# Weight sums of the two-by-two products, made by adding transfers

## The chip, the cores and the metric

The kernel runs on one core of one Trainium2 chip. A core has five engines that run side by side, each with its own queue of instructions, worked off in order: TensorE (PE; matmuls, with the weight loads PEld beside them), VectorE (DVE), ScalarE (ACT), GpSimd (POOL) and SyncE (SP), which here only issues transfers. Transfers issued by any of them run on the core's 16 DMA engines. They wait for each other by semaphores; a framework that lays out the program sets these from what each instruction reads and writes.

The metric is the device time of one execution in microseconds. The kernel before took 825.94 us as the median of three runs (825.88 to 827.58).

## The reference

One layer of an encoder over 512 positions of width 1024, all in float32:

```
h  = rmsnorm(x) * g_pre_mix
q, k, v, g, u, sv, a_ret, a_sgu = split(h @ w_in)
y_ret = (layernorm(retention(q, k, v), both directions) * silu(g)) @ w_ret_o
y_sgu = (gelu(u) * (spatial mixing of layernorm(gelu(sv)))) @ w_sgu_o
merged = sigmoid(a_ret) * y_ret + sigmoid(a_sgu) * y_sgu
x1 = x  + rmsnorm(merged @ w_out) * g_post_mix
y  = x1 + rmsnorm(conv-gated MLP(rmsnorm(x1) * g_pre_ffn)) * g_post_ffn
```

The MLP has a projection up to 2 x 2816 channels, a convolution of width 3 over the positions, gelu(a) * b, and a projection down. Only the matrix products with large weights matter here: `h @ w_in`, the two output projections, `w_out`, `w_up` and `w_down`.

## The kernel before

**Number format.** Every weight tile and every activation is split into a high part (rounded to the format that TensorE multiplies at full rate) and a low part (the rest), and a product is three matmuls: high x high, high x low, low x high. The split (`split`, L84) is one ACT copy (L79) and one VectorE subtraction (L86). So each weight that comes from memory costs ACT and VectorE one pass each before TensorE may use it.

**Weights.** All weights lie in one tensor `wall` of 146 blocks of 128 x 1024 (512 KB). A block is loaded by SP into one of four `raw` tiles and split from there into slots of the pool `w4` (nine of them). `w_get` (L203) hands out the next weight and, while there is room, prepares those that come after it, so splits run ahead of TensorE until the nine slots are full; then a split waits for the matmuls that free a slot.

**Pairs.** For u, for the two gates and for most of the projection up, two blocks of output channels are computed together as one product of two-by-two block matrices with seven products in place of eight (a Strassen-Winograd scheme; `Pair`, L676). The activations come as eight forms (parts of x and the sums S1 to S4), and the weights as seven forms of 128 x 512, in this order:

```
FORMS = ("B11", "B21", "T1", "T2", "T3", "T4", "B22")
```

Here B11, B12, B21, B22 are quarters of the pair's weights, and T1 = B11 + B12, T3 = B12 + B22, T2 = T1 + B22, T4 = T2 + B21. `w_form` (L156) makes them. There are twenty pairs: four of u, eight of the gates, eight couples of the projection up. A pair of u has nothing else beside it; a pair of the gates or of the projection up has two ordinary blocks of weights beside it (`pair[:4]`, block, `pair[4:]`, block, L101 and L106).

A pair's seven products (`part1`: B11, B21, T1, T2; `part2`: T3; `part3`: T4, B22) write to three PSUM banks. Several products add to the same bank: after B11's product ACT copies the bank out (`c0`), T2's product then adds to it, ACT copies again (`c1`), T3's product adds, ACT copies, T4's product adds. Each of these matmuls must wait for the copy before it. For u the `part3` of a pair comes after the `part1` of the next pair.

In the kernel before, the form B11 starts two loads by SP (L160, L161) into raw tiles a and b. The form T1 takes a third raw tile t; VectorE adds T1 and T3 (L167, L168), GpSimd adds T2 (L169), and with the form T4 GpSimd adds T4 (L171). Then each form is split.

**Order.** Each engine's order comes from the framework's scheduler, which starts from the order of the program. GpSimd also does the reciprocal roots of the norms (L322, L325), four loads of xT (L658) just before u, the additions that join the two branches in the second gates (L806), and a few broadcasts. TensorE comes from the product for the gate g into the pairs of u at about 216 us, into the first gates at about 253 us, the second gates at about 367 us, and the couples of the projection up at 520 us.

Of the kernel before, what the change touches and what calls it, by code (L numbers as in the profile page):

```python
# [13 lines left out]
ALU = mybir.AluOpType  # L14

P = 128
D = 1024
S = 512
# [29 lines left out]
def tile_block(ctx: ExitStack, tc, xT, x, wall, par, cs, wsp, bsp, gpost, gffn, out):  # L48
    nc = tc.nc
# [6 lines left out]
    def nm(s):  # L56
        uid[0] += 1
        return f"{s}_{uid[0]}"

    def blk(dt=F32, n="blk", shape=(P, S)):  # L60
        return sb.tile(list(shape), dt, tag="blk", bufs=NBLK, name=nm(n))

    def tmp(n="tmp", shape=(P, S)):
        return sb.tile(list(shape), F32, tag="tmp", bufs=6, name=nm(n))
# [19 lines left out]
    def split(hi, lo, src):  # L84
        copy(hi, src)
        nc.vector.tensor_sub(lo, src, as32(hi))  # L86
# [7 lines left out]
    i = 0  # L94
    while i < NW:
# [7 lines left out]
        elif i == UP0 + 2 * COUPLES[0][0]:  # L103
# [3 lines left out]
            i = UP0 + 2 * COUPLES[-1][1] + 2  # L107
# [10 lines left out]
    w_ready, w_pos, w_held, w_raw = {}, [0, 0], [0], {}  # L118

    def raw_tile():  # L120
        return sb.tile([P, 1024], F32, tag="raw", bufs=4, name=nm("raw"))
# [4 lines left out]
    def slot(n, at=0, w=1024):  # L126
        return sb.tile([P, 1088], F32R, tag="w4", bufs=9, name=nm(n))[:, at : at + w]
# [28 lines left out]
    def w_form(form, i):  # L156

        if form == "B11":
            a, b = raw_tile(), raw_tile()
            nc.sync.dma_start(a, wall[i])  # L160
            nc.sync.dma_start(b, wall[i + 1])  # L161
            w_raw["B11"], w_raw["B12"] = a[:, :S], a[:, S:]
            w_raw["B22"], w_raw["B21"] = b[:, :S], b[:, S:]
        elif form == "T1":
            t = raw_tile()
            w_raw["T1"], w_raw["T2"], w_raw["T3"], w_raw["T4"] = t[:, :S], t[:, S:], w_raw["B12"], t[:, S:]
            nc.vector.tensor_add(w_raw["T1"], w_raw["B11"], w_raw["B12"])  # L167
            nc.vector.tensor_add(w_raw["T3"], w_raw["B12"], w_raw["B22"])  # L168
            nc.gpsimd.tensor_tensor(out=w_raw["T2"], in0=w_raw["T1"], in1=w_raw["B22"], op=ALU.add)  # L169
        elif form == "T4":  # L170
            nc.gpsimd.tensor_tensor(out=w_raw["T4"], in0=w_raw["T2"], in1=w_raw["B21"], op=ALU.add)  # L171
        w = slot("wf", 0, 1088)
        lo, hi = w[:, AT_64 : AT_64 + S], w[:, S + AT_192 : 2 * S + AT_192]
        split(hi, lo, w_raw[form])
        return hi, lo
# [21 lines left out]
    def w_unit(u):  # L197
        return w_block(u[1]) if u[0] == "blk" else (w_down if u[0] in "qt" else w_form)(*u)
# [67 lines left out]
    for k in range(KD):  # L266
# [18 lines left out]
        for m in range(8):  # L285
            c = slice(m * P, (m + 1) * P)
# [5 lines left out]
    T0, T1 = slice(0, 256), slice(256, 512)  # L292
# [35 lines left out]
    for t in range(NT):  # L328
        for n in range(2):
# [3 lines left out]
                out=xt, in_=xt, func=AF.Square, accum_out=ss[:, 4 * n + t : 4 * n + t + 1]  # L333
# [19 lines left out]
    for c in range(19, 1, -2):  # L353
        v.scalar_tensor_tensor(
            out=lc, in0=lc, scalar=1.0 / c, in1=lb, op0=ALU.add, op1=ALU.mult
# [4 lines left out]
        out=lg, in0=lc, scalar=-2.0, in1=lg, op0=ALU.mult, op1=ALU.add  # L360
# [5 lines left out]
    for m in range(8):  # L366
        t = blk(n="qkraw")
# [286 lines left out]
    for n, acc in enumerate(t_group()):  # L654
        if n < 2:
            for k in (n + 2, n + 6):
                t = tmp("xT")
# [83 lines left out]
    for j in range(KD // 2):  # L741
        p = Pair(AF.Gelu_apprx_tanh, lambda: blk(n="u"), None, rbc)
# [52 lines left out]
    for j in range(KD // 2):  # L795
        for o, t in gated_pair(ogh, ogl, late if j == 0 else None):
            b = blk(n="r")
# [221 lines left out]
    i = 0  # L1019
    while i < NF:  # L1020
        if i in couples:
            p = Pair(None, lambda: tmp("c"), (h2h, h2l, h2forms))
# [179 lines left out]
def _parts(a, n, w):  # L1202

    k = a.shape[0] // P
    return a.reshape(k, P, n, w).transpose(2, 1, 0, 3).reshape(n, P, k * w)
# [15 lines left out]
def _two(a):  # L1221

    b = _parts(a, 8, P).reshape(4, 2, P, 2, S)
    return np.stack([
        np.concatenate([b[:, 0, :, 0], b[:, 1, :, 0]], -1), np.concatenate([b[:, 1, :, 1], b[:, 0, :, 1]], -1),
    ], 1)


def _up(a):

    for i, _ in COUPLES:
        b, c = a[2 * i].reshape(P, 2, S), a[2 * i + 1].reshape(P, 2, S)
        a[2 * i : 2 * i + 2] = np.stack([
            np.concatenate([b[:, 0], c[:, 0]], -1), np.concatenate([c[:, 1], b[:, 1]], -1),
        ])
    return a


def _gates(a, w):

    return np.concatenate([_two(a), _parts(w, 8, P).reshape(4, 2, P, 1024)], 1).reshape(16, P, 1024)
# [79 lines left out]
```

## Time and profile before

| what | value |
|---|---|
| median of three runs | 825.94 us (825.88 to 827.58) |
| the profiled execution | 827.49 us, of which the span of the profile is 825.7 us |
| granted TensorE clock | 0.999 |
| busy: TensorE, VectorE, ScalarE, GpSimd | 815.4, 661.4, 440.8, 101.0 us |
| HBM read, written | 88.19 MB, 4.19 MB |
| loads of raw tiles by SP | 145 of 512 KB, median 3.6 us to landing |

Rows of a group read: line, engine, operation, what it writes and reads, shapes, count, then busy time in us and the mean of one in ns, then the engine's idle time just before and what ended it. The chain of work that ended last gives start, length and the piece; several instructions of one line in a row are one piece (x48: 48 of them). The timeline gives start, length, engine, line, and in brackets the idle time before and its end. A wait reads: who waited, for whom, total us, times, longest. A DMA issue gives count, size and the median time from issue to landing. Time runs from the span's start.

### The profile page before, as it was taken

What the parts mean: (1) busy time and instruction counts of PE and PEld (TensorE: products, weight loads), DVE (VectorE), ACT (ScalarE), POOL (GpSimd) and SP (SyncE); (2) the same over time, 40 slices, a digit from 0 to 9 for tenths busy, and PEclk for the clock granted to TensorE, in tenths of its full rate; (3) what the DMA queues carried; (4) which work ended last, traced back from release to release, by engine and by line L of the source; (5) the groups of instructions that cost most, each with busy time, mean ns of one, the idle gap of its engine ahead of it and who ended that gap; (6) DMA issues with size and microseconds to landing.
All of it is one profiled execution on the core that took longest, in us unless ns stands there. A gap on an engine that the chain in (4) does not pass through costs nothing.

```text
span 825.7 us, 13263 instructions
## 1 busy us (share of the span) xinstructions
PE 815.4 (99%) x5152; PEld 735.0 (89%) x5152; DVE 661.4 (80%) x1101; ACT 440.8 (53%) x771; POOL 101.0 (12%) x102
## 2 busy tenths in 40 slices
PE   9999999999999999999999999999999999999996
PEld 7888888888899999999988898899999998999996
DVE  7489897878797777767765568979899899988967
ACT  6636445546665444444445685556566566544531
POOL 0010000102121111132211211210111200000001
PEclk9999999999999999999999999999999999999999
DMA  8733222212223232222349111322322341233244
GB/s 294 246 116 102 77 77 77 77 52 78 90 102 129 103 102 80 101 101 103 108 166 339 48 55 55 103 102 103 102 103 102 102 154 52 77 115 129 96 147 154
DMA packets 29215, 93.24 MB, mean 113 GB/s; under 512 B 3360, under 2 KB 4000, under 8 KB 29152
## 3 DMA queue, kind: packets, MB, share of 16 engines
q1 hardware_dynamic: 26928, 86.85, 30.2%
q0 software_dynamic: 1360, 4.46, 1.6%
q10 hardware_dynamic: 864, 1.09, 0.4%
q8 instruction: 40, 0.66, 0.3%
q14 instruction: 23, 0.19, 0.1%
HBM read 88.19 MB, written 4.19 MB: 112 GB/s over the span
## 4 chain that ended last, share of the span: by engine, by line
PE 91%; DVE 6%; ACT 1%; issue 1%; DMA 0%; POOL 0%; DVEq 0%; SPq 0%; POOLq 0%; ACTq 0%
PE ps L692 23%; PE ps L217 12%; PE ps L218 12%; PE ps L219 12%; PE ps L1058 8%; PE ps L481 5%; PE ps L480 5%; PE ps L482 5%; PE ps L836 2%; PE ps L837 2%; PE ps L838 2%; PE ps L1074 1%; PE ps L761 1%; DVE fl L86 1%; PE ps L279 1%
## 5 line engine op out<-in xcount | busy, mean ns | idle before, releaser
L86 DVE TENSOR_TENSOR wl<-raw,wh 128x1024 fp32r<-128x1024 f32 (+1 forms) x93 | 109.1, 1182 | 48.9 <-PE ps L692 24.2
L79 ACT ACTIVATE wf<-raw 128x512 fp32r<-128x512 f32 x140 | 85.3, 627 | 102.7 <-PE ps L218 34.0
L86 DVE TENSOR_TENSOR wf<-raw,wf 128x512 fp32r<-128x512 f32 x140 | 111.1, 808 | 23.3 <-ACT wf L79 22.4
L692 PE MATMUL ps<-sh,wf 128*128 128x256 f32 x640 | 119.5, 277 | 0.0
L79 ACT ACTIVATE wh<-raw 128x1024 fp32r<-128x1024 f32 (+2 forms) x95 | 93.3, 993 | 37.4 <-DMA raw<-wall 17.0
L692 PEld LDWEIGHTS ps<-sh,wf 128*128 128x128 f32 x640 | 101.1, 188 | 0.8 <-ACT u L79 0.2
L217 PE MATMUL ps<-h2h,wh 128*128 128x512 f32 (+1 forms) x256 | 92.4, 363 | 0.7 <-ACT h2h L906 0.7
L218 PE MATMUL ps<-h2l,wh 128*128 128x512 f32 (+1 forms) x256 | 92.4, 363 | 0.0
L219 PE MATMUL ps<-h2h,wl 128*128 128x512 f32 (+1 forms) x256 | 92.1, 361 | 0.0
L692 PE MATMUL ps<-sl,wf 128*128 128x256 f32 x320 | 88.8, 278 | 0.0
L480 PE MATMUL ps<-wh,xh 128*128 128x512 f32 x192 | 75.0, 391 | 0.0
L481 PE MATMUL ps<-wl,xh 128*128 128x512 f32 x192 | 74.9, 390 | 0.0
L482 PE MATMUL ps<-wh,xl 128*128 128x512 f32 x192 | 74.8, 390 | 0.0
L169 POOL TENSOR_TENSOR raw<-raw,raw 128x512 f32<-128x512 f32 x20 | 36.2, 1809 | 235.2 <-DVE raw L167 207.8
L1058 PE MATMUL ps<-dl,fh 128*128 128x256 f32 x216 | 60.8, 281 | 0.1
L1058 PE MATMUL ps<-dh,fl 128*128 128x256 f32 x216 | 60.7, 281 | 0.0
L1058 PE MATMUL ps<-dh,fh 128*128 128x256 f32 x216 | 60.7, 281 | 0.0
L692 PEld LDWEIGHTS ps<-sl,wf 128*128 128x128 f32 x320 | 60.0, 188 | 0.6
L219 PEld LDWEIGHTS ps<-h2h,wl 128*128 128x128 f32 x256 | 48.0, 188 | 7.7
L217 PEld LDWEIGHTS ps<-h2h,wh 128*128 128x128 f32 x256 | 47.9, 188 | 7.9 <-ACT h2h L906 1.0
L692 PE MATMUL ps<-xh,wf 128*128 128x256 f32 x288 | 54.2, 278 | 0.0
L218 PEld LDWEIGHTS ps<-h2l,wh 128*128 128x128 f32 x256 | 48.0, 188 | 6.6
(314 smaller groups left out, 2048.9 us busy)
## 6 DMA issues: line engine op xcount, KB each, us to landing
raw<-wall SPq DMA_DIRECT2D x145, 512.0 KB, 3.6
x<-x SPq DMA_DIRECT2D x24, 256.0 KB, 5.9
xT<-xT SPq DMA_DIRECT2D x8, 256.0 KB, 5.4
x<-x POOLq DMA_DIRECT2D x8, 256.0 KB, 2.4
xT<-xT POOLq DMA_DIRECT2D x4, 256.0 KB, 3.6
out<-zg SPq DMA_DIRECT2D x4, 256.0 KB, 2.0
out<-zs ACTq DMA_DIRECT2D x3, 256.0 KB, 3.5
cs<-cs SPq DMA_DIRECT2D x2, 256.0 KB, 4.1
```

The lines of the kernel that those rows point to most:

```text
L79: nc.scalar.activation(out=o, in_=i, func=AF.Copy)
L86: nc.vector.tensor_sub(lo, src, as32(hi))
L169: nc.gpsimd.tensor_tensor(out=w_raw["T2"], in0=w_raw["T1"], in1=w_raw["B22"], op=ALU.add)
L217: nc.tensor.matmul(o, ah, bh, start=start, stop=False)
L218: nc.tensor.matmul(o, ah, bl, start=False, stop=False)
L219: nc.tensor.matmul(o, al, bh, start=False, stop=stop)
L480: nc.tensor.matmul(acc[t], xh[k][:, c], wh[:, f], start=k == 0, stop=False)
L481: nc.tensor.matmul(acc[t], xh[k][:, c], wl[:, f], start=False, stop=False)
L482: nc.tensor.matmul(acc[t], xl[k][:, c], wh[:, f], start=False, stop=k == KD - 1)
L692: nc.tensor.matmul(o, w_[:, c], a_, start=first and k == n == 0, stop=k == 3 and n == 2, skip_group_check=True,)
L836: nc.tensor.matmul(o, ah, bh, start=k == 0, stop=False)
L1058: nc.tensor.matmul(o, a_[:, c], w_[:, f], start=j == t == i == 0, stop=j == DP - 1 and i == 2 and n not in (M2, M3, M4), skip_group_check= ...
```

## The change

The weights are laid out otherwise in memory, so that a pair's first block is B11|B21 and its second is B12|B22 (`_two`, `_up`). With the form B11 three raw tiles are taken at once, t, a and b, in this order:

- SP loads t = B11|B12, the left halves of both blocks, by one transfer with two rows of 2 KB for each partition. GpSimd issues a transfer that adds the second block, B12|B22, to it: t = T1|T3.
- SP loads a = B11|B21.
- SP loads b = B22|B22, one half block read twice. GpSimd issues a transfer that adds T1, from t, to b's right half: b = B22|T2.
- With the form T1 GpSimd issues a transfer that adds T2, from b, to a's right half: a = B11|T4. It must wait until B21 has been split.

The four additions on VectorE and GpSimd are gone. The matmuls, the splits and the forms' order are the same. In the changed program GpSimd's queue has, for the pairs of u, the T1|T3 sum of the next pair ahead of the T4 sum of this one; for later pairs the three sums of a pair stand together. The first T1|T3 sum stands ahead of the last reciprocal root of the retention, the first T2 sum ahead of the loads of xT. TensorE's order of matmuls is the same; ScalarE's and VectorE's differ in a few neighbours. Below the changed lines, line numbers are one lower than before.

```diff
         if form == "B11":
-            a, b = raw_tile(), raw_tile()
+            t, a, b = raw_tile(), raw_tile(), raw_tile()
+            nc.sync.dma_start(t.rearrange("p (b c) -> p b c", b=2), wall[i : i + 2, :, :S].rearrange("b p c -> p b c"))
+            nc.gpsimd.dma_start(t, wall[i + 1], accum_op=ALU.add)
             nc.sync.dma_start(a, wall[i])
-            nc.sync.dma_start(b, wall[i + 1])
-            w_raw["B11"], w_raw["B12"] = a[:, :S], a[:, S:]
-            w_raw["B22"], w_raw["B21"] = b[:, :S], b[:, S:]
+            twice = wall[i + 1, :, None, S:].to_broadcast([P, 2, S])
+            nc.sync.dma_start(b.rearrange("p (b c) -> p b c", b=2), twice)
+            nc.gpsimd.dma_start(b[:, S:], t[:, :S], accum_op=ALU.add)
+            w_raw["T1"], w_raw["T3"] = t[:, :S], t[:, S:]
+            w_raw["B11"], w_raw["B21"] = a[:, :S], a[:, S:]
+            w_raw["B22"], w_raw["T2"], w_raw["T4"] = b[:, :S], b[:, S:], w_raw["B21"]
         elif form == "T1":
-            t = raw_tile()
-            w_raw["T1"], w_raw["T2"], w_raw["T3"], w_raw["T4"] = t[:, :S], t[:, S:], w_raw["B12"], t[:, S:]
-            nc.vector.tensor_add(w_raw["T1"], w_raw["B11"], w_raw["B12"])
-            nc.vector.tensor_add(w_raw["T3"], w_raw["B12"], w_raw["B22"])
-            nc.gpsimd.tensor_tensor(out=w_raw["T2"], in0=w_raw["T1"], in1=w_raw["B22"], op=ALU.add)
-        elif form == "T4":
-            nc.gpsimd.tensor_tensor(out=w_raw["T4"], in0=w_raw["T2"], in1=w_raw["B21"], op=ALU.add)
+            nc.gpsimd.dma_start(w_raw["T4"], w_raw["T2"], accum_op=ALU.add)
...
     return np.stack([
-        np.concatenate([b[:, 0, :, 0], b[:, 1, :, 0]], -1), np.concatenate([b[:, 1, :, 1], b[:, 0, :, 1]], -1),
+        np.concatenate([b[:, 0, :, 0], b[:, 0, :, 1]], -1), np.concatenate([b[:, 1, :, 0], b[:, 1, :, 1]], -1),
     ], 1)
...
         a[2 * i : 2 * i + 2] = np.stack([
-            np.concatenate([b[:, 0], c[:, 0]], -1), np.concatenate([c[:, 1], b[:, 1]], -1),
+            np.concatenate([b[:, 0], b[:, 1]], -1), np.concatenate([c[:, 0], c[:, 1]], -1),
         ])
```

In the changed kernel the three adding transfers are L161 (T1|T3), L165 (T2) and L170 (T4), the three loads L160, L162 and L164.

## The prediction

> **What bounds the kernel now.** I read the cores first, then the busy time per engine, then what TensorE waited for, and last the chain that ended last around the pairs.
>
> ```profile
> core 0: 825.7 us, clock 0.999
> PE 815.4 (99%) x5152; PEld 735.0 (89%) x5152; DVE 661.4 (80%) x1101; ACT 440.8 (53%) x771; POOL 101.0 (12%) x102
> PE ps L264 <- DVE raw L259: 1.0, 1, 1.0
> PE ps L217 <- ACT h2h L906: 0.7, 1, 0.7
> PE ps L624 <- DVE o L615: 0.3, 1, 0.3
> PE ps L605 <- DVE o L615: 0.3, 1, 0.3
> 216.77 5.92 PE ps L692 x52
> 222.72 39.74 PE ps L692 x332
> 561.55 5.45 PE ps L692 x48
> 582.05 5.45 PE ps L692 x48
> ```
>
> TensorE is busy for 815.4 of 825.7 us at full clock, and all that it waited for by name is a handful of waits of 1.0 us at most; the rest of its idle time is the end of the kernel. So work taken off VectorE or GpSimd is worth next to nothing as such. What the change can do is make TensorE wait. The place to look is where pairs follow one another fastest: the four pairs of u with the first four products of the gate run from 216.77 to 222.72 + 39.74 = 262.46, 384 matmuls in 45.7 us, so 32 products at 1.43 us and a pair in 10.0 us. A later pair has two ordinary blocks beside it: from the first products of one couple of up to those of the next it is 20.5 us (561.55 to 582.05).
>
> **What it removes.**
>
> ```profile
> L167 DVE TENSOR_TENSOR raw<-raw 128x512 f32<-128x512 f32 x20 | 13.8, 688 | 1.5 <-DMA raw<-wall 1.4
> L168 DVE TENSOR_TENSOR raw<-raw,raw 128x512 f32<-128x512 f32 x20 | 17.1, 853 | 1.0 <-DMA raw<-wall 0.7
> L169 POOL TENSOR_TENSOR raw<-raw,raw 128x512 f32<-128x512 f32 x20 | 36.2, 1809 | 235.2 <-DVE raw L167 207.8
> L171 POOL TENSOR_TENSOR raw<-raw,raw 128x512 f32<-128x512 f32 x20 | 26.7, 1333 | 75.2 <-DVE wf L86 71.4 <-ACT cv L955 3.9
> L86 DVE TENSOR_TENSOR wf<-raw,wf x140: 674/686/1782, 191.9 to 668.1; 128x512 fp32r<-128x512 f32 x140
> ```
>
> VectorE loses 13.8 + 17.1 = 30.9 us, GpSimd 36.2 + 26.7 = 62.9 us, and VectorE's splits no longer meet a GpSimd sum (686 ns is the usual split, 1782 the one beside such a sum). Of all this the path sees one thing: TensorE's wait of 0.3 us for L615, which has L167 and L168 ahead of it on VectorE. Gain: 0.3 us. What is late next there is the release of the slots by TensorE itself.
>
> **What it adds.** Per pair, SP issues three loads of 512 KB for two; GpSimd issues three adding transfers: T1|T3 (512 KB from wall, on t), T2 (256 KB, from t on b), T4 (256 KB, from b on a). Twenty pairs move 31 MB more.
>
> ```profile
> q1 hardware_dynamic: 26928, 86.85, 30.2%
> raw<-wall SPq DMA_DIRECT2D x145, 512.0 KB, 3.6
> x<-x POOLq DMA_DIRECT2D x8, 256.0 KB, 2.4
> xT<-xT POOLq DMA_DIRECT2D x4, 256.0 KB, 3.6
> DMA to landing us min/median/max: 3.3/3.6/6.8
> 188.00 2.38 POOL L658 DMA_DIRECT2D xT<-xT  x4
> ```
>
> 60 issues at 0.6 us (four in 2.38) are 36 us on a GpSimd that has just lost 62.9: hidden. Twenty more SP issues at 0.33 us fall on a queue that mostly waits. The engines stand at 30.2% of 825.7 us x 16 for 86.85 MB, or 45.9 engine-us per MB, so 512 KB takes 1.5 us on all sixteen; 31 MB more is no bound on the average. Latency is what counts.
>
> No transfer of before adds. Call x the time of the 256 KB one from issue to landing, X that of the 512 KB one. Ends for x: 2.4 (the GpSimd queue's stores, same size) and 6.8 (the slowest load of raw). I take x = 3.6, the GpSimd queue's row of the same size that also writes a tile: that it must read its target too (0.75 us by the rate above) and that its source is on the chip (2.4 against 3.6) roughly cancel. For X I take 3.6 + 1.5 = 5.1, the load of that size and its second read; ends 3.6 and 6.8. The Trainium skill, page "DMA: Bandwidth & Descriptors", section "Anatomy of one DMA", fits 2.0 us + bytes/436e3 for a transfer of this queue, which is 2.6 us for 256 KB. The xT row has 3.6 for that size, so the trace is a microsecond above it.
>
> **The pairs of u.** Four raw tiles turn in the order t, a, b, t, a, b, so b of a pair lies in the tile of the a before it, whose right half holds the former T4. That makes a ring: T4 is split, SP loads b into its place (3.6), GpSimd adds t (x), GpSimd adds it on a (x), the new T4 is split. On TensorE's side the ring has 10.0 us.
>
> ```profile
> 209.16 1.30 DVE L86 TENSOR_TENSOR wf<-raw,wf 128x512 fp32r<-128x512 f32 x2 [2.45 <-ACT wf L79]
> 222.56 0.62 ACT L79 ACTIVATE wf<-raw 128x512 fp32r<-128x512 f32 x1
> 223.22 0.69 DVE L86 TENSOR_TENSOR wf<-raw,wf 128x512 fp32r<-128x512 f32 x1 [0.20 <-ACT wf L79]
> 243.00 0.63 ACT L79 ACTIVATE wf<-raw 128x512 fp32r<-128x512 f32 x1 [0.42 <-POOL raw L171]
> 245.15 0.37 ACT L79 ACTIVATE u<-ps 128x256 f32<-128x256 f32 x1
> 256.05 0.37 ACT L79 ACTIVATE sig<-ps 128x256 f32<-128x256 f32 x1
> ```
>
> T4 of the first pair is split as before (209.16, the first of two), so the second pair's b can be loaded from 210; its T4 is split on time too, being summed by 213.6 + 2x = 220.8, before ACT wants it at 222.56. VectorE is done at 223.9, and from 224.0 on: third pair's T4 at 224.0 + 3.6 + 2x; with 1.5 for the two halves of the split and the hand-over, the fourth's at 224.0 + 2(3.6) + 1.5 + 4x = 232.7 + 4x, that of the first gate pair at 237.8 + 6x. At x = 3.6 these are 234.8, 247.1 and 259.4, where ACT had 243.00 for the fourth.
>
> TensorE uses T4 late, but ACT runs in order, and behind the T4 split stands the copy of the pair's first product out of its bank (245.15 and 256.05), which must be done before the T2 product adds to that bank. T2 of the fourth pair starts with matmul 264 of the 384, at 222.72 + 212 x 0.1197 = 248.1; T2 of the gate pair with 348, at 258.15. The fourth pair's copy ends 1.6 us after its T4 (splits of T4 and B22, then itself): 234.3 + 4x against 248.1. The gate pair's ends 1.05 after: 238.85 + 6x against 258.15. So TensorE loses 6x - 19.3 by then, if x is over 3.2: at x = 3.6 it is **2.3 us**; at 2.4 nothing, at 6.8 21.5. The splits themselves keep 1 us or more ahead of their products, so the copies are what is late.
>
> **The gates.** From the split of T4 it now goes: load of the next t (3.6), X, then x for T2, and behind the T2 split on ACT stands the copy of the T3 product, due before the T4 product (the x24 pieces of the chain).
>
> ```profile
> 300.55 0.68 DVE L86 TENSOR_TENSOR wf<-raw,wf 128x512 fp32r<-128x512 f32 x1
> 313.95 0.38 ACT L79 ACTIVATE sig<-ps 128x256 f32<-128x256 f32 x1 [0.44 <-PE ps L692]
> 316.66 2.73 PE ps L692 x24
> 387.12 3.00 POOL L806 TENSOR_TENSOR sig<-sig,r 128x512 f32<-128x512 f32 x2 [6.28 <-DVE sig L805]
> 389.00 0.33 SPq L161 DMA_DIRECT2D raw<-wall  x1
> 399.55 0.38 ACT L79 ACTIVATE sig<-ps 128x256 f32<-128x256 f32 x1 [0.39 <-PE ps L692]
> 402.26 2.73 PE ps L692 x24
> ```
>
> First four pairs: t can load from 301.3, lands 304.9; the copy must start by 316.2, the T2 split by 315.6: X + x may be 10.7. It is 5.1 + 3.6 = 8.7, and a and b loading at the same moment add perhaps 0.5: hidden. Second four, without the mixing of the SGU in between: t from 389.05 (where SP went on when the split was done), landed 392.65; T2 must be split from 401.2: X + x may be 8.55, and 9.2 is 0.65 too much, at three passages from pair to pair: **2.0 us**. GpSimd's sums of the branches (L806) end at 390.1, before it waits for t; behind its three transfers nothing else is due. On SP the load of b, waiting for its tile, holds back only the loads of the next tiles, which are wanted later.
>
> **The couples of up.** There the copy of the T3 product stands ahead of the splits of T1 and T2, and the couple lasts 20.5 us:
>
> ```profile
> 573.87 0.38 ACT L79 ACTIVATE c<-ps 128x256 f32<-128x256 f32 x1 [1.29 <-PE ps L692]
> 576.23 0.63 ACT L79 ACTIVATE wf<-raw 128x512 fp32r<-128x512 f32 x1 [1.24 <-POOL raw L169]
> ```
>
> T2's split at 576.23 is used only after the next couple begins, 582.05; I count nothing, up to about 4 us of delay.
>
> **Moved on GpSimd's queue.** Its first adding transfer stands ahead of a reciprocal root, its second ahead of the loads of xT.
>
> ```profile
> 171.01 0.33 SPq L160 DMA_DIRECT2D raw<-wall  x1
> 180.60 0.20 POOL L322 TENSOR_SCALAR rs<-mv 128x4 f32<-128x4 f32 x1 [16.11 <-DVE mv L559]
> 184.22 1.22 DVE L86 TENSOR_TENSOR wl<-raw,wh 128x1024 fp32r<-128x1024 f32 x1 [0.91 <-PE ps L481]
> 194.88 1.35 ACT L255 ACTIVATE xg<-xT,part 128x512 f32<-128x512 f32 x2
> ```
>
> t lands by 174.6, so the root is not held. b's tile comes free when the ordinary block before is split (184.22 + 1.22) and lands by 189.2, so xT goes out at 189.8 for 188.0 and lands by 193.4; ACT wants it at 194.88. Hidden, with 1.5 us left; beyond that every microsecond delays the forms of x.
>
> **Sum.** -0.3 + 2.3 + 2.0 = +4.0 us. The profiled execution took 827.49 us (span 825.7 and 1.8 around it), so 831.5 on its account; it lies at the top of the three runs (825.88 to 827.58). On their median, 825.94, it is 829.9.
>
> **Rivals.** *Hidden: no change.* An adding transfer takes 3.2 us or less and X + x no more than 8.0. The place is the ring of u: up to x = 3.2 it costs nothing, and only the 0.3 us is left: 825.6. For it: the GpSimd queue's stores, 2.4. Against it: the loads of that queue have 3.6, and this one reads two things. By the fit of the Trainium skill's page x would be 2.6, the ring would hide it, and the sum would be -0.3. *Slow adding.* The engines need four times the pass of a plain copy: x = 3.6 + 1.5 = 5.1, X = 3.6 + 3.0 = 6.6. Then u costs 11.3; the first gates 12.2 - 10.7 = 1.5 at four passages, 6; the second 3.65 at three, 11: 854. For it: nothing in this trace adds in flight, so nothing excludes it; against it, the loads are mostly fixed time (3.6, of which 1.5 moves bytes). *Faster.* VectorE and GpSimd get 94 us lighter. TensorE's waits after the start add up to 1.3 us (0.7, 0.3 and one of 0.3 more), so this ends at 824.6 at best, inside what can be told.
>
> **How the numbers follow.** Under 0.2% (1.65 us) a measurement can't tell this kernel from no change. Stalls as forecast 0.48 (its own range 827.6 to 842: x from 3.5 to 5), hidden 0.30, slow adding 0.17, faster 0.05. Slower is the first, the third and a little of the second: 0.67; same 0.29, with most of the rival that gains; faster 0.04. The range 825.2 to 845 leaves out most of the slow case and the gains.
>
> **What would show it.** L165 and L170 landing near 3.6 us and L161 near 5. ACT's wf splits of T4 released by a DMA around 235, 247 and 259, and TensorE waiting for ACT u and sig in L692, 2 to 3 us before 262; three waits for ACT sig between 380 and 425. VectorE near 610 us busy (661.4 less 30.9 and the stretched splits). Wrong, if the adding transfers land over 5 us (then waits in all gates), or if TensorE waits for wf itself, or if the xT forms are late before 216.

## The result, and the profile after

The changed kernel takes 868.81 us as the median of four runs (865.83 to 870.79), against 825.99 for the kernel before in the same comparison (825.88 to 827.58): 1.052 times as long, 95% interval 1.0479 to 1.056. The forecast was 829.9, with a range to 845. The profiled execution took 870.79 us, its span 869.0.

The busy rows of the changed kernel's page:

```profile
PE 830.3 (96%) x5152; PEld 745.1 (86%) x5152; DVE 617.0 (71%) x1061; ACT 438.7 (50%) x771; POOL 90.4 (10%) x122
```

What TensorE waited for by name (who, for whom, total us, times, longest):

```profile
PE ps L691 <- ACT c L79: 11.7, 7, 4.5
PE ps L691 <- ACT sig L79: 11.3, 7, 3.8
PE ps L691 <- ACT u L79: 6.0, 2, 3.9
PE ps L623 <- DVE o L614: 0.3, 1, 0.3
```

VectorE did get lighter (661.4 to 617.0). TensorE now waits 29 us for the copies of ScalarE out of the banks, in 16 stalls of u, the gates and up; none of these rows names a wf tile. The same matmuls also take 830.3 us instead of 815.4. The wait of 0.3 for the transposes (L623; L624 before) is still there.

Both kernels issue the same 5152 matmuls in the same order, so the start of the n-th in one trace less its start in the other says how late a stage begins. That gives where the 43.3 us went: u with the first gate pair 16.3, the rest of the first gates 2.5, the second gates 7.9, up 17.0; nothing before u, nothing between the second gates and up, nothing after.

The issues of transfers (count, KB, median us to landing):

```profile
raw<-wall SPq DMA_DIRECT2D x165, 512.0 KB, 4.1
raw<-wall POOLq DMA_DIRECT2D x20, 512.0 KB, 6.6
raw<-raw POOLq DMA_DIRECT2D x40, 256.0 KB, 3.3
```

The landings of the line of T1|T3 (L161) and then of b (L164):

```profile
DMA to landing us min/median/max: 5.4/6.6/9.4
DMA to landing us min/median/max: 3.9/5.5/8.3
```

The page's row of the queue that adds (packets, MB, share of the 16 engines' time):

```profile
q0 software_dynamic: 10000, 25.43, 15.6%
```

The 256 KB adding transfer (x) takes 3.3 us, a little less than forecast; the 512 KB one (X) 6.6 where 5.1 was forecast, and up to 9.4; the load of b 5.5 where 3.6 was.

One turn of the ring of u, in the timeline of the changed kernel (start, length, engine, line; in brackets the idle time before and what ended it). L164 loads b, L165 adds T2, L161 adds the next pair's T1|T3, L170 adds T4, and L79 is the split:

```profile
240.81 0.37 SPq L164 DMA_DIRECT2D raw<-wall  x1
245.30 0.85 POOL L165 DMA_DIRECT2D raw<-raw  x1 [9.48 <-DVE wf L86]
246.86 0.86 POOL L161 DMA_DIRECT2D raw<-wall  x1 [0.70 <-DVE u L728]
249.16 0.87 POOL L170 DMA_DIRECT2D raw<-raw  x1 [1.43 <-issue]
253.75 1.15 ACT L79 ACTIVATE wf<-raw 128x512 fp32r<-128x512 f32 x2 [1.42 <-DMA raw<-raw]
255.13 0.37 SPq L164 DMA_DIRECT2D raw<-wall  x1
```

From load to load it is 4.5 us for b and the hand-over to GpSimd, 3.9 for T2 and the next hand-over, 4.6 for T4 (the next T1|T3 runs beside it), 1.4 for the split: 14.3 us, where 12.3 was forecast and TensorE has 10.0.

And one couple of up, from one stalled T4 product to the next (TensorE's rows are the first matmul of that product):

```profile
590.45 0.58 PE L691 MATMUL ps<-h2h,wf 128*128 128x256 f32 x1 [1.98 <-ACT c L79]
595.11 0.64 ACT L79 ACTIVATE wf<-raw 128x512 fp32r<-128x512 f32 x1 [0.46 <-PE ps L691]
596.50 0.38 SPq L160 DMA_DIRECT2D raw<-wall  x1
600.82 0.88 POOL L161 DMA_DIRECT2D raw<-wall  x1 [9.93 <-DVE cv L961]
608.27 0.86 POOL L165 DMA_DIRECT2D raw<-raw  x1 [6.57 <-DVE gp L986]
613.03 0.63 ACT L79 ACTIVATE wf<-raw 128x512 fp32r<-128x512 f32 x1 [3.83 <-DMA raw<-raw]
613.56 0.37 ACT L79 ACTIVATE c<-ps 128x256 f32<-128x256 f32 x1
613.98 0.39 PE L691 MATMUL ps<-h2h,wf 128*128 128x256 f32 x1 [1.12 <-ACT c L79]
```

T4's product frees a slot, the next T4 is split into it (595.11), that frees the tile for the next t (596.50), then X, b's arrival and T2 follow, ACT splits T2 (613.03), and only then comes the copy of the T3 product that TensorE's T4 product waits for. This too is a ring: 23.5 us, where the couple had 20.5 before. Its copy stands behind the T2 split on ACT.

### The profile page after: what moved, and what is told of

Same layout as the page of the kernel before. It is cut to its first block, busy times and chain, and to the rows that moved or that the text cites. A ratio compares the mean times of both kernels' runs of the same rounds, so it can differ in the third digit from the quotient of the medians.

```text
span 869.0 us, 13395 instructions
## 1 busy us (share of the span) xinstructions
PE 830.3 (96%) x5152; PEld 745.1 (86%) x5152; DVE 617.0 (71%) x1061; ACT 438.7 (50%) x771; POOL 90.4 (10%) x122
## 3 DMA queue, kind: packets, MB, share of 16 engines
q0 software_dynamic: 10000, 25.43, 15.6%
## 5 line engine op out<-in xcount | busy, mean ns | idle before, releaser
L86 DVE TENSOR_TENSOR wf<-raw,wf 128x512 fp32r<-128x512 f32 x140 | 99.3, 717 | 116.2 <-ACT wf L79 115.8
L79 ACT ACTIVATE wf<-raw 128x512 fp32r<-128x512 f32 x140 | 85.4, 626 | 157.8 <-DMA raw<-raw 61.3
L86 DVE TENSOR_TENSOR wl<-raw,wh 128x1024 fp32r<-128x1024 f32 (+1 forms) x93 | 106.3, 1152 | 37.0 <-ACT wh L79 14.8
L691 PE MATMUL ps<-sh,wf 128*128 128x256 f32 x640 | 124.5, 284 | 7.5 <-ACT u L79 6.0
L691 PEld LDWEIGHTS ps<-sh,wf 128*128 128x128 f32 x640 | 105.1, 194 | 8.9 <-ACT u L79 6.6
L79 ACT ACTIVATE wh<-raw 128x1024 fp32r<-128x1024 f32 (+2 forms) x95 | 93.2, 991 | 36.3 <-DMA raw<-wall 15.8
L691 PE MATMUL ps<-sl,wf 128*128 128x256 f32 x320 | 90.8, 284 | 0.0
L691 PE MATMUL ps<-xh,wf 128*128 128x256 f32 x288 | 58.2, 292 | 9.7 <-ACT sig L79 9.7
L691 PEld LDWEIGHTS ps<-sl,wf 128*128 128x128 f32 x320 | 62.2, 194 | 0.6
L691 PEld LDWEIGHTS ps<-xh,wf 128*128 128x128 f32 x288 | 48.6, 200 | 12.5 <-ACT sig L79 12.3
```

The costliest lines, as they stand in the source:

```text
L79: nc.scalar.activation(out=o, in_=i, func=AF.Copy)
L691: nc.tensor.matmul(o, w_[:, c], a_, start=first and k == n == 0, stop=k == 3 and n == 2, skip_group_check=True,)
```

## The experiments

Time, ratio to before with its 95% interval, and by how many us each stage delayed the matmuls in the profiled execution, against the profiled execution of before (in e7 the added matmuls are left out of the count). What is gained or lost behind up, up to 3 us either way, is left out. The first two numbers are of all runs, the stages of one execution: in the changed kernel, e9, e10, e11 and e14 that was the slowest of its runs, in e5 the fastest. What is lost ahead of u in e1, e2, e8 and e9 begins with TensorE waiting 2.1 to 4.4 us in all (0.6 before) for VectorE's output of the retention (o, L614 in the changed kernel). "Chain" is the theory that the sums come late one behind another, with ACT in order behind them; the rivals stand with each run.

| run | us | ratio | ahead of u | u, first gate pair | first gates | second gates | up |
|---|---|---|---|---|---|---|---|
| changed | 868.81 | 1.052 (1.0479-1.056) | -0.3 | 16.3 | 2.5 | 7.9 | 17.0 |
| e1 T1, T3 on VectorE | 833.75 | 1.0105 (1.0077-1.0134) | 1.9 | 7.2 | 0 | 0 | 0 |
| e2 T2, T4 on GpSimd | 836.92 | 1.015 (1.0114-1.0187) | 2.5 | 5.8 | 0 | 1.3 | 1.6 |
| e3 six tiles | 831.81 | 1.008 (1.0053-1.0107) | -0.2 | 6.7 | 0 | 0 | -0.1 |
| e4 copies, not sums | 835.52 | 1.0128 (1.0083-1.0172) | -0.4 | 7.3 | 0 | 0.9 | 1.8 |
| e5 copy first | 844.5 | 1.0235 (1.0207-1.0263) | 0.2 | 12.4 | 0 | 4.3 | 0.4 |
| e6 u on engines | 862.37 | 1.0454 (1.0419-1.049) | -0.7 | 11.2 | 4.6 | 7.1 | 13.0 |
| e7 stalls filled | 873.39 | 1.0585 (1.0562-1.0608) | 0.2 | 15.1 | 4.7 | 9.8 | 16.9 |
| e8 six tiles, u on engines | 833.57 | 1.0109 (1.0086-1.0131) | 3.6 | 5.0 | 0 | 0 | -0.4 |
| e9 three loads, no adding transfer | 841.29 | 1.0192 (1.017-1.0213) | 4.8 | 7.1 | 0 | 0 | 5.9 |
| e10 copy first in u too | 843.05 | 1.0231 (1.0209-1.0252) | -0.1 | 12.6 | 1.3 | 5.6 | 1.5 |
| e11 up alone, copy first | 831.31 | 1.0086 (1.0059-1.0113) | -0.8 | 1.7 | 0 | 0 | 10.2 |
| e12 six tiles, copies | 826.08 | 1.0018 (1.0004-1.0031) | -0.7 | -1.2 | 0 | 0 | -0.4 |
| e13 e9 with six tiles | 830.21 | 1.0065 (1.0042-1.0088) | -0.5 | 2.9 | 0 | 0 | -0.1 |
| e14 five tiles | 850.12 | 1.0304 (1.0277-1.033) | 1.7 | 10.1 | 0 | 0.6 | 11.6 |

### e1 and e2: one link of the chain taken out

e1:

```diff
-            nc.gpsimd.dma_start(t, wall[i + 1], accum_op=ALU.add)
...
+            nc.vector.tensor_add(t[:, :S], t[:, :S], t[:, S:])
+            nc.vector.tensor_add(t[:, S:], t[:, S:], b[:, :S])
             nc.gpsimd.dma_start(b[:, S:], t[:, :S], accum_op=ALU.add)
```

> The 512 KB adding transfer is taken out: T1 and T3 are added in place by VectorE (about 0.7 and 0.85 us each) once t and b have landed; all loads and the two adding transfers of T2 and T4 stay. Theory of the chain (sums late one behind another, and ACT in order behind them): the ring of u (load of b, T2, T4) does not contain the removed transfer, so it stays at 13 to 14 us a pair and u still loses 8 to 12 us; in the gates and in up T1 comes some 6 us earlier, so the stalls there (9 in the second gates, 11 in up and what the clock loses behind them) go: 838 to 845 us. Rival, the shared transfer engines: with a third of the added traffic gone every stage gains in proportion, u too, and the time falls to 832 or less. If neither L161 nor the traffic matters it stays near 869.

e2:

```diff
-            nc.gpsimd.dma_start(b[:, S:], t[:, :S], accum_op=ALU.add)
...
-            nc.gpsimd.dma_start(w_raw["T4"], w_raw["T2"], accum_op=ALU.add)
+            nc.gpsimd.tensor_tensor(out=w_raw["T2"], in0=w_raw["T1"], in1=w_raw["T2"], op=ALU.add)
+        elif form == "T4":
+            nc.gpsimd.tensor_tensor(out=w_raw["T4"], in0=w_raw["T2"], in1=w_raw["T4"], op=ALU.add)
```

> The two 256 KB adding transfers are taken out: GpSimd adds T2 and T4 in place (1.3 to 1.8 us each); the three loads and the 512 KB adding transfer stay. Theory of the chain: the ring of u falls to 5 + 1.8 + 1.3 + 1.5 = 9.6 us and u loses nothing or little (0 to 3); in the gates T2 still has the load of t and the 512 KB transfer in front (4 + 7 to 9, then 1.8: 13 to 15 us against the 12.2 that the second gates allow), so 1 to 3 us at each of three passages there, a little in up: 830 to 840 us. Rival, the shared engines: the 512 KB transfers are the larger part of the added traffic, they stay, and so does over half of the loss: 845 us or more.

By the ratios either link alone brings back 34 and 31 of the 43 us (1.052 less 1.0105 and 1.015, times 826), so the loss is no sum over transfers: it is what a chain exceeds its interval by, pair after pair. In the gates and in up nearly all goes with either; u keeps 6 to 7 in both. e2's time lies in the chain's range, but not by the chain's terms: u lost 5.8 where it allowed 0 to 3, and the gates lost less than it had. e1 fell between the two expectations, u having lost 7.2 where the ring alone had 8 to 12.

### e4: the same transfers without adding

```diff
-            nc.gpsimd.dma_start(t, wall[i + 1], accum_op=ALU.add)
+            nc.gpsimd.dma_start(t, wall[i + 1])
```

and likewise for the other two.

> The changed kernel whose three extra transfers copy instead of adding (the sums are left out, so T1 to T4 are not the reference's): same bytes from the source, same queue, same waits. If adding itself is what makes them slow, the 512 KB one falls from 6.6 us to 4 or 5, the 256 KB ones from 3.3 to 2.5, and the time to 835 to 850 us. If the length is that of any transfer of this queue beside the loads, the landings stay within 10% and the time at 860 to 870 us.

The issues of e4, to be read beside 6.6 and 3.3, and its row of that queue, beside 15.6%:

```profile
raw<-wall POOLq DMA_DIRECT2D x20, 512.0 KB, 5.0
raw<-raw POOLq DMA_DIRECT2D x40, 256.0 KB, 2.3
```

```profile
q0 software_dynamic: 7440, 25.43, 8.9%
```

Adding costs 1.6 us for 512 KB and 1.0 for 256 KB, 3.6 us over a pair's three. It takes the engines about twice as long for the same bytes (15.6% of 869.0 us against 8.9% of 835.2, each with the 1.6% of 825.7 that this queue had before the change). The copies are also issued in 0.53 us instead of 0.86. These 4 to 5 us of chain are worth 32 us of time; the rival, landings within 10%, falls.

### e3, e14, e12: six and five tiles

```diff
-        return sb.tile([P, 1024], F32, tag="raw", bufs=4, name=nm("raw"))
+        return sb.tile([P, 1024], F32, tag="raw", bufs=6, name=nm("raw"))
```

with `NBLK = 72` (e14: five and 74; e12: six, and the copies of e4).

> The changed kernel with six tiles for raw weights instead of four (and 72 instead of 76 block tiles, for the room). Theory of the chain through four tiles: t, a and b of a pair no longer wait for the pair before, the three transfers run up to a pair ahead, and nearly all of the loss goes: 826 to 834 us, if the four block tiles are not missed. Rival, the shared engines: in u the transfers of a pair keep all engines busy for 0.72 x 46 us / 3.1 pairs = 10.7 us against TensorE's 10.0, and landing times grow with the overlap: u still loses 3 us or more and the rest part of its stalls: 840 to 855 us.

> The changed kernel with five tiles for raw weights (74 block tiles). With five, the next t but one takes the place of a T4 in u, and in the gates and in up the next t takes the place of t itself, free when T3 is split, a few us ahead of T4. Theory of the ring: in u a period of (4.4 + 7.5 + 4.2 + 4.2 + 1.5) / 2 = 10.9 us against 10.0, so 3 us lost there with what the shared engines add up to 7; in the gates and in up 3 us or more of room, so stalls shrink to a few of 1 us: 832 to 842 us, between four tiles (869) and six (832). Rival (only the full two pairs of tiles help): 855 us or more.

> Six tiles for raw weights, and the three extra transfers copy instead of adding (the sums are left out, so T1 to T4 are not the reference's). Theory (with six tiles u is bound by the shared engines, of which an adding transfer takes twice the time of a copy: 16.6% against 8.9% for that queue): u loses 3 us or less instead of 6.5: 825 to 828.5 us. Rival (another wait bounds u there): it still loses 5 or more: 830 us or more.

With six tiles the rings are cut: the gates and up lose nothing, as the chain has it. Only u does, as the shared engines have it. From 222 to 252 us (columns: busy of the five engines with counts, granted clock, share of the DMA engines, GB/s), in e3 and then in e12:

```profile
222.00:252.00 30.00, 26.20 (x223) 25.59 (x221) 15.77 (x28) 14.57 (x29) 5.16 (x6) 1.00 0.89 210
```

```profile
222.00:252.00 30.00, 29.98 (x265) 29.78 (x264) 21.39 (x39) 19.78 (x37) 4.13 (x8) 1.00 0.73 237
```

In e3 the DMA engines are at 0.89, in single stretches at 1.0, and TensorE stands. The T2 and T4 transfers take 5.5 and 4.3 us as medians over the kernel. The T4 transfer that ScalarE waits for ahead of e3's longest stall in u (3.5 us) took 8.5:

```profile
250.69 0.63 ACT L79 ACTIVATE wf<-raw 128x512 fp32r<-128x512 f32 x1 [6.59 <-DMA raw<-raw]
```

With copies, which move as many bytes, the engines stand at 0.73 and TensorE runs through. So with four tiles the ring bounds u, with six the engines, by the double time of adding. e12 also shows that the block tiles given up for the room (72 for 76) are not missed. Five tiles gave 850.12, between the two as the rings have it but above my 842: u lost 10.1 and up 11.6, 3.2 of that in the work just ahead of up. What a fifth tile frees I had not worked out well enough.

### e5 and e10: the copy ahead of the late splits

```diff
+                after["T1"] = after["T2"] = c.ins
...
-        split(hi, lo, w_raw[form])
+        with tc.issue_after(after[form]) if form in after else ExitStack():
+            split(hi, lo, w_raw[form])
```

where `c` is the copy of the T3 product; and T1 and T2 of the next pair are asked for one product later (`w_get(3.5)`). e5 does not part these two. e10 does the same for a T4 of u and the first copy of the next pair.

> The changed kernel with one order on ScalarE turned round in the gates and in up: the copy of the T3 product out of its bank stands ahead of the splits of the next pair's T1 and T2 (which are also asked for one product later); u is as it was. Theory (the sums are late for the copy behind them, not for their own products): the stalls in front of the T4 products, 21 us, and most of the slow clock behind them go; u's part of 11 us stays: 836 to 842 us. Rival (the sums are late for their own products too): TensorE then waits for the wf tiles of T1 or T2 instead, and the time stays above 852.

> The order of the run before (copy of the T3 product ahead of the splits of T1 and T2 in the gates and in up), and now also in u: the copy of a pair's first product stands ahead of the split of the T4 of the pair before. Theory of the ring (load of b, T2, T4, split: 14 to 15 us a pair, and no copy in it): the order does not help, TensorE waits a little later for a wf tile of T4 instead, and u still loses 8 us or more of its 12.6: 839 to 845 us. Rival (it is the copies behind the split that are late): u loses 4 us or less: 831 to 836 us.

In e5 the stalls ahead of the T4 products are gone, and with them 2.5 us in the first gates and 16.6 of 17.0 in up; TensorE waits for no wf tile. Of the 11.7 us that it waited for the copies of up (tile `c`) this is left:

```profile
PE ps L692 <- ACT c L79: 0.2, 1, 0.2
```

The median, 844.5, is 2.5 us above what I expected; the profiled execution, at 841.99, is not. In its second gates two new stalls of 1.6 and 2.1 us stand ahead of T2 products, which wait for the copy of their pair's first product. In the timeline of ScalarE, one couple: copy first, then T1, and T2 after a wait of 2.06 us that nobody feels:

```profile
591.19 0.38 ACT L79 ACTIVATE c<-ps 128x256 f32<-128x256 f32 x1 [0.58 <-PE ps L692]
591.47 0.62 ACT L79 ACTIVATE wf<-raw 128x512 fp32r<-128x512 f32 x1
594.16 0.63 ACT L79 ACTIVATE wf<-raw 128x512 fp32r<-128x512 f32 x1 [2.06 <-DMA raw<-raw]
```

In u the order changes nothing (12.4 and 12.6), and the loads of b still follow each other in e10 after 15.6 and 14.7 us (SP's queue at 227.44, 243.02, 257.68). That is the ring, and no copy stands in it. The wait for a wf tile that I expected in e10 did not come: the longest stalls of u move from the T2 products to the T3 products, which wait for the copy after T2, and that copy now stands behind the T4 split (in one turn 241.64 for the split, 245.24 for the copy). So in up, and for the stalls of the T4 products in the gates, it was the place of the copy; in u it was the ring.

### e6, e8, e11: parts of the change

`w_form` takes for some pairs the two loads and the four sums on the engines, as before the change: for u (e6), for u with six tiles (e8), for u and the gates with e5's order (e11).

> The four pairs of u are summed on VectorE and GpSimd from two loads, as before the change; gates and up as changed. Theory (each stage's chain is too long for its own interval): u's 11 us go, and the 13 stalls in front of T4 products stay, about 21 us and 8 of slow clock less what the first passage loses by starting on time: 846 to 855 us. Rival (the later stalls are lateness carried over from u): 835 or less.

> Six tiles for raw weights (72 block tiles), u summed on the engines from two loads as before, gates and up by adding transfers. Theory (what is left of the loss with six tiles is u alone, where the transfers of a pair fill the engines): no stall is left, within 0.2% of before, 824 to 826 us on this chip. Rival (six tiles only hide the stages one after the other, or the block tiles are missed): 828 us or more.

> Adding transfers for the eight couples of up alone, with the copy of the T3 product ahead of the splits of T1 and T2; the pairs of u and of the gates are summed on the engines from two loads, as before. Theory: with that order up hides its transfers (0.4 us lost in the run with the copy first), so this is within 0.2% of before: 824 to 826.5 us on this chip. Rival (up loses by them whatever the order): 828 us or more.

e6 refutes that the later stalls are carried over from u: they stay. It lost 7 us more than I expected, since the passage from u to the first gate pair costs 11.2 us by itself. TensorE stands there for 4.3 us at the T2 product of u's last pair: on ScalarE the copy that it needs is behind a split that waited 3.0 us for the gate pair's load a, which SP issued only at 245.99.

e8 gained nothing over e3, against my forecast, and its trace shows two other causes. Ahead of u (3.6 us) TensorE waited 2.0 us for VectorE's last output of the retention, which came after a sum of weights of 1.8 us; the matmuls behind that wait were 1.8 us slower. In u (5.0 us) the mixture itself is at fault: GpSimd works in order, and the T4 sum of a pair of u (L172) stands there behind the T2 transfer of the first gate pair (L180), which waited for a T1|T3 that took 8.05 us to land. ScalarE waited for that sum, with the copy for TensorE behind it:

```profile
250.04 0.88 POOL L180 DMA_DIRECT2D raw<-raw  x1 [7.69 <-DMA raw<-wall]
250.65 1.59 POOL L172 TENSOR_TENSOR raw<-raw,raw 128x512 f32<-128x512 f32 x1
252.27 0.63 ACT L79 ACTIVATE wf<-raw 128x512 fp32r<-128x512 f32 x1 [6.38 <-POOL raw L172]
```

So e8 does not test whether u alone is what six tiles leave; that the gates and up lose nothing, it does show.

e11 missed too: with the copy first, up lost 0.4 us in e5 but 10.2 here, in the slowest of six runs (827.07 to 835.97). Its landings of the T1|T3 transfer, and TensorE's wait for the copies in up:

```profile
DMA to landing us min/median/max: 5.6/7.3/9.5
```

```profile
PE ps L707 <- ACT c L79: 6.2, 4, 2.8
```

The order in e11 is that of e5, and its four stalls stand ahead of T2 products, like those of e5 in the second gates. The two long ones follow T1|T3 transfers that took 9.0 and 9.5 us: ScalarE waited 2.9 and 2.6 us for T1 and then 3.2 and 3.4 for T2, and reached the copy of the next couple's first product too late. So the turned order leaves up at the edge, not hidden.

When T1|T3 lands late can be read from the issues. In the gates and in up of the changed kernel and of e5, ten of the thirty T1|T3 transfers had the load of b issued 1.2 us or more behind them, and took 5.3 to 6.6 us; the other twenty, with that load closer or ahead, took 6.5 to 9.4. In e11 it is 5.6 for two and 6.4 to 9.5 for six. Why b's load came closer in e11 than in e5 stays open.

### e7: idle matmuls in the stalls

```diff
+            fill = {5: 24, 10: 26, 13: 32, 14: 10}.get(self.number, 0)
...
+            for _ in range(fill):
+                nc.tensor.matmul(self.b[1][:, T1], i16[:, 0:P], i16, start=True, stop=True, skip_group_check=True)
```

> The changed kernel with 24, 26, 32 and 10 idle matmuls (bf16, 128x256, into an unused half of a bank) in front of the T4 products of the first gate pair, the sixth, and the first two couples of up, where TensorE stands for 3.5, 3.8, 4.5 and 2.0 us. Theory (TensorE's own idleness lowers its clock behind a stall): the granted clock right behind these stalls stays at 1.00 where it read 0.66 to 0.75, and some 7 of the 869 us go: 860 to 864 us. Rival (the low clock has another cause): it stays low and the time at 867 to 871 us.

The three microseconds behind the stall at 404 (same columns as above), in the changed kernel and then in e7:

```profile
405.00:408.00 3.00, 3.00 (x16) 3.00 (x15) 0.92 (x1) 0.00 (x0) 0.00 (x0) 0.50 0.54 93
```

```profile
405.00:408.00 3.00, 2.96 (x24) 2.96 (x25) 1.95 (x4) 0.94 (x1) 0.46 (x1) 1.00 0.51 87
```

Sixteen matmuls at a clock of 0.50 became 24 at 1.00, and likewise behind the other three: the idleness lowers the clock. But the time did not fall; it is 873.39, where I had written down 7 us of gain. Later stalls grew instead: the last two of the first gates from 0.6 and 0.4 us to 1.2 and 1.8, that of the seventh gate pair from 0.85 to 4.1. As I read it, the sums set the pace, and TensorE's slow microseconds lie inside the time that it would wait anyway. e7 filled only four stalls; whether the rest of the 15 us of longer matmuls cost anything was not tried.

### e9 and e13: three loads and no adding transfer

T1 and T3 as in e1, T2 and T4 as in e2; e13 with six tiles.

> The three loads of the changed kernel stay (t, a, and b with its right block read twice), but all four sums are made on the engines, T1 and T3 by VectorE, T2 and T4 by GpSimd; no transfer adds. Theory (what costs time is the length of the chain of adding transfers): the ring of u is 5 + 1.8 + 1.3 + 1.5 = 9.6 us against 10.0, nothing is lost: 824 to 828 us on this chip. Rival (the third load and the double reading are what u loses 5 to 7 us by, since it lost that much whichever sum was taken out): 830 to 834 us.

> The three loads of the changed kernel with all sums on the engines, as in the run that lost 16 us without an adding transfer, but with six tiles for raw weights (72 block tiles). Theory (that loss is the ring through the four tiles: b can only be loaded into the place of the T4 of the pair before): the ring is gone and the time is that of before to 0.4%: 824 to 828 us. Rival (the third load, or VectorE and GpSimd taking sums in place in that order, cost it): 834 us or more.

My 9.6 us for the ring was wrong. SP issues the loads of b in e9 at

```profile
229.29 0.37 SPq L163 DMA_DIRECT2D raw<-wall  x1
242.26 0.37 SPq L163 DMA_DIRECT2D raw<-wall  x1
254.39 0.37 SPq L163 DMA_DIRECT2D raw<-wall  x1
```

which is 13.0 and 12.1 us a turn. As I read VectorE's timeline, it takes its sums in order among the splits, and splits beside a GpSimd sum take 1.75 us. So 16 us are lost without any adding transfer; my rival's 830 to 834 was missed as well. With six tiles u loses 2.9 and the rest nothing: it was the ring through the tiles, b loaded into the place of a T4, and the third load as such costs little. The time is 830.21, 0.65% above before, where I had expected 828 at most.

No run is faster than the kernel before, whose TensorE is busy 99% of its span; of those that compute the reference, e13 and e3 come nearest.

## Why the prediction was wrong, step by step

**What bounds the kernel.** Right: lighter VectorE and GpSimd brought nothing (617.0 us of VectorE, forecast 610), and what counts is whether TensorE is made to wait. The 0.3 us for L615 did not go.

**The prices.** x = 3.6 was nearly right as a median (3.3), but in the ring of u, beside the next pair's T1|T3, T4 took 4.4 to 5.1. X = 5.1 was too low: 6.6, and 5.0 even for a plain copy. The loads had 3.6: t has a median of 4.4 and b of 5.5. "a and b loading at the same moment add perhaps 0.5" was the term for neighbours: T1|T3 took 5.4 to 6.6 us in the gates and in up where b's load followed by 1.2 us or more, and 6.5 to 9.4 elsewhere. And a step was left out: from landing to the next issue on GpSimd, 0.6 us at each of the hand-overs. This is the first failed step: X + x and the loads were priced by rows in which few transfers ran beside each other, and the ring without hand-overs.

The rival of slow adding had 6.6 for X, and that it came out is luck: it had 5.1 for x and "four times the pass", where e4 shows about twice. Its sums, moreover, add two passes to the plain transfer's one, which makes three.

**u.** The mechanism was right: the ring through b, T4's splits released by transfers (forecast at 235, 247, 259; traced at 239.43, 253.75, 267.54), TensorE waiting for u and sig. The period was 14.3 us instead of 12.3: 0.9 more for b with its hand-over, 0.3 for T2, 1.0 for T4. The overrun adds up turn by turn. TensorE stood first at the T2 product of the third pair (3.9 us), a turn earlier than forecast, and 2.3 us became 10.9 by the T2 product of the gate pair.

**The gates.** The passage from u was not seen as the place where a chain made for 20 us meets 10: 5.4 us at the first T4 product of the gates. In the second gates the form of the sum was right. In the timeline of the changed kernel:

```profile
384.45 0.38 SPq L160 DMA_DIRECT2D raw<-wall  x1
389.63 0.88 POOL L161 DMA_DIRECT2D raw<-wall  x1 [1.50 <-DMA raw<-wall]
399.21 0.63 ACT L79 ACTIVATE wf<-raw 128x512 fp32r<-128x512 f32 x1 [6.54 <-DMA raw<-wall]
403.11 0.63 ACT L79 ACTIVATE wf<-raw 128x512 fp32r<-128x512 f32 x1 [3.26 <-DMA raw<-raw]
403.64 0.37 ACT L79 ACTIVATE sig<-ps 128x256 f32<-128x256 f32 x1
404.06 0.58 PE L691 MATMUL ps<-xh,wf 128*128 128x256 f32 x1 [3.82 <-ACT sig L79]
```

5.2 us from the load of t to the adding transfer (forecast 3.6), 9.6 to the split of T1 (forecast 5.1), 3.9 to that of T2 (3.6): 6.4 us more than the terms of the forecast, on top of the 0.65 that it had as overrun. The load of t began 2.7 us earlier before the T4 product than in the forecast, which takes some of it back; TensorE stood for 3.8. The second gates came to 7.9 us where 2.0 was forecast.

**Up.** The second failed step: "There the copy of the T3 product stands ahead of the splits of T1 and T2". I read it from one couple (573.87). In the ScalarE timeline of before the copy stands behind the T2 split in four of seven passages, where the sums came early enough for it not to matter, and in all seven of the changed kernel. One of the four, with T1, T2 and then the copy:

```profile
592.78 0.63 ACT L79 ACTIVATE wf<-raw 128x512 fp32r<-128x512 f32 x1 [3.81 <-DVE raw L168]
593.95 0.63 ACT L79 ACTIVATE wf<-raw 128x512 fp32r<-128x512 f32 x1 [0.54 <-POOL raw L169]
594.49 0.37 ACT L79 ACTIVATE c<-ps 128x256 f32<-128x256 f32 x1
```

That is 17.0 us counted as nothing; e5 shows it by taking 16.6 of them away. Of the 39 us that the forecast was short in the profiled execution, up has these 17, u with the first gate pair 14 and the other gates 8.

**xT, the root, SP's queue.** No delay at the start of u, as forecast (TensorE is 0.3 us early), but not by the terms of the forecast. xT went out at 191.17 instead of 189.8 and took 6.6 to 7.8 us beside T2 and the next t, where 3.6 was priced. ScalarE had to wait for it:

```profile
197.76 0.72 ACT L254 ACTIVATE xg<-xT,part 128x512 f32<-128x512 f32 x1 [2.45 <-DMA xT<-xT]
```

That is 2.9 us later than before, past the 1.5 us of room, and one of the prediction's own signs of being wrong. That TensorE did not feel it is luck, since the forecast had given the forms of x no such room.

**What was not thought of.** The granted clock of 0.50 behind stalls (filling four of them gained nothing, by e7), and that a ring in every stage turns small overruns into losses for each pair.

## What to carry to other kernels

When a sum moves from an engine to a transfer, follow the tile: list what must be free before its load, what must land before its sum, and what stands behind its first reader on that engine; if that closes into a ring, its period against TensorE's interval decides, and every microsecond above is paid once per turn. Price each link beside the transfers that the change itself starts, not by the quiet rows of before. Read an order that your argument rests on from every turn, since a scheduler does not repeat itself.

## What the runs showed of the hardware

- **Adding in flight.** On GpSimd's queue 512 KB from memory took 6.6 us adding and 5.0 copying, 256 KB within the chip 3.3 and 2.3, with about twice the engine time. An adding issue holds GpSimd for 0.86 us, a copying one for 0.53. These are medians beside the loads of this kernel; with b's load issued at nearly the same time the 512 KB took up to 9.4.
- **The clock behind a stall.** Over the profiled executions of all kernels but e7 I took the stalls of 0.4 to 4.5 us with no other within the next 45 matmuls, and how much longer those 45 took than in before. About 70 stalls of up to 1.96 us: at most 0.45 us. 23 stalls of 2.17 us and more: 1.1 to 2.65 us, most 1.5 to 1.75. Of six between 1.98 and 2.09 four lost 1.6 to 1.8 and two 0.1. The Trainium skill, page "TensorE: Matmul & The Clock Gate", section "What's actually happening", has half the clock after an idle window of about 3.4 us. The 0.50 agrees; the length does not: here 2.2 us of standing was always enough, and the measurement decides.
